# Modulation columns: the last gate of each layer summed over row tiles by VectorE, the first group of columns on a later unit

## The chip, the cores and the metric

One NeuronCore of a Trainium2 chip runs the whole program, one launch. The metric is the device time of one execution in microseconds (us). Before the change the median of three runs is 1773.07 us (1772.1 to 1774.9).

## The reference, cut to what matters

One inference step of a two-layer backbone. 128 context tokens and 256 latent tokens of width D = 1024 go through the same layers with different conditioning vectors (`c_ctx` and `c`). In each layer:

```python
mod = (silu(cond) @ w_mod[l] + b_mod[l]).reshape(B, 9, 1, 1024)
sh1, sc1, gt1, sh2, sc2, gt2, sh3, sc3, gt3 = [mod[:, i] for i in range(9)]
h = rmsnorm(x, g0) * (1 + sc1) + sh1;  x = x + 0.5 * gt1 * swiglu(h, w1[0], w2[0])
h = rmsnorm(x, g1) * (1 + sc2) + sh2;  x = x + gt2 * mixer(h)
h = rmsnorm(x, g2) * (1 + sc3) + sh3;  x = x + 0.5 * gt3 * swiglu(h, w1[1], w2[1])
```

The nine vectors sh1 to gt3 are the modulation. `w_mod[l]` is 1024 x 9216 in fp32. Vector i stands in columns i*D to (i+1)*D, so sh1 and sc1 are columns 0 to 2D, gt2 is 5D to 6D, and the last gate gt3 is 8D to 9D. It multiplies the output of the second feed-forward (FFN2), so it is needed when FFN2's second product comes out. Outputs are the normed tokens and the final states of the context scan. Everything is fp32.

## The kernel before, in words

**Main work.** Tokens are kept transposed, as 8 tiles `x0` to `x7` of 128 channels by 384 tokens. A weight unit is 512 KB (128 x 1024 fp32, mostly four row tiles by 256 columns). SyncE's queue (SP) loads it into `wr` (L149), ScalarE (ACT) copies the rounded high part to `wh` (L126), VectorE (DVE) subtracts to get the low part `wl` (L105), and TensorE (PE) runs three products per row tile and 128 columns, `mm3` (L198 to L200): high by high, high by low, low by high. A unit gives 24 matmuls. Units are prepared two ahead. The activations are split in the same way into `hh` and `hl`.

**Order.** PE follows the written program order. On DVE, ACT and the DMA queues a scheduler chooses the order when the program is built, by priority and by its own idea of times; each engine then runs its list strictly in order, and SP too. From the fourth unit on (`settled`) weight loads, and the loads of `mod_cols` and `mod_half`, carry a high priority (`ahead()`); the loads of `mod_wide` (L433) do not.

**Side work.** Everything but the big products is written as generators that are hung on `tracks`. `track(gen, rate, start)` sets a counter to -start*rate; after each unit `tick()` adds the rate, and each whole 1.0 lets the generator take one step. So rates and starts place the side work between the units.

**Modulation** is made in three ways.

- `mod_half`: columns 0 to 2D of layer 0, two halves, before and during the first units. Per row tile k one 512 KB load (L373; tiles k > 3 in another pool) and four matmuls (`band_products`, L356): silu(cond) against four column bands, each band into its own 32 rows of a bank.
- `mod_cols`: groups of up to 1536 columns (`MG`), two row tiles per step. A step loads two 128 x 1536 tiles (768 KB each, L394), one step ahead if `early_loads`, and then runs the four bands of each tile on PE (the trace records 16 matmuls per step). After four steps `mod_out` copies the bank out (ACT, L460), transposes it on PE and adds the bias.
- `mod_wide`: 1024 columns. Eight 512 KB loads (L433); for each row tile two accumulations on DVE, one per conditioning vector, `macc` (L123, 128 x 1024; the first row tile is done by ACT, L436); then PE sums over the 128 rows with eight small matmuls against a `pick` tile (L444, 16 records), and `mod_out`.

The loads of `modw` tiles share a pool of four buffers (`m6`): a load waits at the head of SP until the product or accumulation that read the buffer's last content is done.

**Norms.** Each residual update of `x` is followed by a square on ACT (L503) and an addition into `sqacc` on DVE (L105). When `x7` is done, PE sums `sqacc` over the channels (`token_sums`, L486), ACT and DVE make `rstd` (L522) and `diag` (L118), and PE broadcasts it (L533). PE meanwhile runs the next layer part's first products on the unnormed `xh`, `xl`.

**At the start**, PE first has the first half of columns 0 to 2D, then runs the products of row tiles 0 to 3 of units 0 and 1, with the second half's band products put between them; then it needs `hh4` to `hh7` (L639), which need the second half's scale `sc`.

Of the kernel before, what the change touches and what calls it, by code (L numbers as in the profile page):

```python
# [4 lines left out]

# [16 lines left out]
D = 1024  # L22
# [10 lines left out]
NMOD = 9  # L33
# [16 lines left out]
MG = 1536  # L50
# [6 lines left out]
def hybrid_step(ctx: ExitStack, tc: tile.TileContext, I, pos_r, pos_c, y_prompt, y_sample, new_state):  # L57
# [20 lines left out]
    def ax_bank():  # L78
        return ps_ax.tile([P, 512], F32, tag="ax", name="ax")
# [18 lines left out]
    def m6(shape, name, dt=F32):  # L98
        return mx.tile(shape, dt, tag="m6", name=name, bufs=4)
# [43 lines left out]
    def ahead():  # L143
        return nullcontext() if early["on"] else tc.high_priority()
# [73 lines left out]
    def track(gen, rate, start=0):  # L218
        tracks.append([gen, rate, -start * rate])
# [134 lines left out]
    def band_products(b, k, raw, w):  # L354
        for s in range(4):
            pe.matmul(  # L356
                b[32 * s : 32 * s + 32, :w],
                silu_c[:, k, :],
                raw[:, s * w : s * w + w],
                start=(k == 0),  # L360
                stop=(k == KD - 1),
                skip_group_check=True,
            )
# [21 lines left out]
    def mod_cols(l, c0, c1, early_loads=True):  # L385

        steps = [(c, min(MG, c1 - c), k) for c in range(c0, c1, MG) for k in range(0, KD, 2)]

        def load(c, n, k0):
            raws = []  # L390
            for k in (k0, k0 + 1):
                raw = m6([P, n], "modw")
                with ahead():
                    nc.sync.dma_start(raw, I["w_mod"][l][k * P : (k + 1) * P, c : c + n])  # L394
                raws.append(raw)
            return raws

        nxt = load(*steps[0]) if early_loads else None
        yield
        for i, (c, n, k0) in enumerate(steps):  # L400
            raws = nxt if early_loads else load(c, n, k0)
            if early_loads and i + 1 < len(steps):
                nxt = load(*steps[i + 1])
            yield
            if k0 == 0:
                b = ax_bank()
            for j in range(2):
                band_products(b, k0 + j, raws[j], n // 4)
            yield
            if k0 == KD - 2:  # L410
                yield from mod_out(l, b, [c + s * (n // 4) for s in range(4)], n // 4)
                mod_done(l, c, n)

    def mod_done(l, c0, n):

        for i in range(NMOD):
            if c0 < (i + 1) * D <= c0 + n:
                if i % 3 == 1:
                    norm_scale(l, i // 3)
                elif i % 3 == 2:  # L420
                    gate_scale(l, i // 3)
# [6 lines left out]
    def mod_wide(l, c0, n=WU):  # L428

        acc = [c4([P, WU], f"macc{s}") for s in range(2)]  # L430
        for k in range(KD):
            raw = m6([P, WU], "modw")
            nc.sync.dma_start(raw, I["w_mod"][l][k * P : (k + 1) * P, c0 : c0 + WU])  # L433
            for s in range(2):
                if k == 0:
                    act.activation(acc[s], raw, AF.Copy, scale=silu_c[:, k, s : s + 1])  # L436
                else:
                    stt(acc[s], raw, silu_c[:, k, s : s + 1], acc[s])
                yield
        w = WU // 4  # L440
        b = ax_bank()
        for i in range(2):
            for s in range(4):
                pe.matmul(  # L444
                    b[32 * s : 32 * s + 32, :w],
                    pick[:, i, :],
                    acc[i][:, s * w : (s + 1) * w],
                    start=(i == 0),
                    stop=(i == 1),
                    skip_group_check=True,  # L450
                )
        yield
        yield from mod_out(l, b, [c0 + s * w for s in range(4)], w)
        mod_done(l, c0, n)
        yield

    def mod_out(l, b, starts, w):
        nb = w // P
        ev = sp.tile([P, 512], F32, tag="c2", name="modev", bufs=7)
        act.activation(ev[:, :w], b[:, :w], AF.Copy)  # L460
        yield
        b2 = ax_bank()
        for j in range(nb):
            transpose(b2[:, j * P : (j + 1) * P], ev[:, j * P : (j + 1) * P], P)
        src = b2[:, :w].rearrange("p (b s r) -> p b s r", s=4, r=32)
        for s, c0 in enumerate(starts):
            j0 = c0 // P
            bias = bm_t[l][:, j0 : j0 + nb].unsqueeze(2).to_broadcast([P, nb, 2])
            add(mod_t[l][:, j0 : j0 + nb, :], src[:, :, s, 0:2], bias)
# [1195 lines left out]
    def mod_wides(l, c0, c1):  # L1665
        for c in range(c0, c1, WU):
            yield from mod_wide(l, c)

    def tables(l):
        if l == 0:  # L1670
            yield from s5_params(*s5_params_in(nc.gpsimd))
        yield from s5_tables(l)
# [97 lines left out]
    track(other_vectors(), 0.25, 8)  # L1770
    for l in range(DEPTH):
        if l == 0:
            track(mod_cols(0, 2 * D, 8 * D), 0.7)
            track(tables(0), 1.9, 8)
        else:
            track(tables(1), 1.6, 8)
            track(mod_cols(1, 6 * D, NMOD * D), 0.36, 10)
        nxt = Lead(l, 1)
        ffn(l, 0, 0, ld, nxt, None if l else more)
        ld, nxt = nxt, Lead(l, 2)  # L1780
        mixer(l, ld, nxt)
        if l == 0:
            track(mod_cols(0, 8 * D, NMOD * D, False), 1.0)
            track(mod_cols(1, 0, 2 * D, False), 0.5, 14)
            track(mod_wides(1, 2 * D, 6 * D), 1.2, 4)
        ld, nxt = nxt, Lead(l + 1, 0) if l + 1 < DEPTH else Final()
        ffn(l, 1, 2, ld, nxt)
        ld = nxt
# [59 lines left out]
```

## Time and profile before

| | |
|---|---|
| median of three runs | 1773.07 us |
| profiled execution | 1772.74 us |
| its span in the trace | 1770.9 us |
| mean granted clock of PE, share of full speed | 0.994 |
| PE / DVE / ACT busy, share of the span | 98% / 71% / 45% |
| DMA, mean over the span | 195 GB/s |

The span is the part that the trace covers; the execution's own time is 1.8 us longer. PE is busy nearly always. Where it is idle or runs at half clock is the first 50 us. One more matmul on PE, or one less, is therefore a change of the end, unless it falls into a wait.

### The profile page before, as it was taken

What the parts mean: (1) busy time and instruction counts of PE and PEld (TensorE: products, weight loads), DVE (VectorE), ACT (ScalarE), POOL (GpSimd) and SP (SyncE); (2) the same over time, 40 slices, a digit from 0 to 9 for tenths busy, and PEclk for the clock granted to TensorE, in tenths of its full rate; (3) what the DMA queues carried; (4) which work ended last, traced back from release to release, by engine and by line L of the source; (5) the groups of instructions that cost most, each with busy time, mean ns of one, the idle gap of its engine ahead of it and who ended that gap; (6) DMA issues with size and microseconds to landing.
All of it is one profiled execution on the core that took longest, in us unless ns stands there. A gap on an engine that the chain in (4) does not pass through costs nothing.

```text
span 1770.9 us, 31161 instructions
## 1 busy us (share of the span) xinstructions
PE 1739.2 (98%) x12244; PEld 1660.3 (94%) x12244; DVE 1249.3 (71%) x2352; ACT 795.7 (45%) x1332; POOL 202.6 (11%) x400
## 2 busy tenths in 40 slices
PE   6999999999999999999999999999999999999997
PEld 4989989999999999999999999999999999999997
DVE  5495776888986986657787666677699688544445
ACT  3344333475355553233367333335744546323233
POOL 2012333410010000000001133222100000000000
PEclk9999999999999999999999999999999999999999
DMA  9679787676753567766745577757666443444342
GB/s 358 209 234 317 251 261 213 204 213 188 251 150 102 185 223 247 255 197 219 250 131 184 174 220 233 244 172 236 167 209 195 131 126 113 135 128 128 122 125 77
DMA packets 250298, 344.49 MB, mean 195 GB/s; under 512 B 22016, under 2 KB 216268, under 8 KB 250153
## 3 DMA queue, kind: packets, MB, share of 16 engines
q1 hardware_dynamic: 225048, 299.18, 53.1%
q0 software_dynamic: 17088, 39.51, 7.4%
q10 hardware_dynamic: 8016, 3.82, 0.8%
q8 instruction: 96, 1.57, 0.4%
q14 instruction: 50, 0.40, 0.1%
HBM read 309.75 MB, written 32.70 MB: 193 GB/s over the span
## 4 chain that ended last, share of the span: by engine, by line
PE 84%; DVE 10%; DMA 2%; ACT 2%; issue 1%; DVEq 0%; SPq 0%; ACTq 0%
PE mm L198 26%; PE mm L200 26%; PE mm L199 26%; PE ax L356 3%; DVE wl L105 2%; DVE cacc L123 2%; PE tb L138 1%; DVE m_t L105 1%; DMA wr<-in_w_in_dram 1%; DVE m_hh L105 1%; DMA wr<-in_w_gate_dram 1%; ACT wh L126 1%; PE tb L1042 0%; DMA modw<-in_w_mod_dram 0%; DVE acc L105 0%
## 5 line engine op out<-in xcount | busy, mean ns | idle before, releaser
L105 DVE TENSOR_TENSOR wl<-wr,wh 128x1024 fp32r<-128x1024 f32 (+2 forms) x389 | 457.0, 1175 | 335.7 <-ACT wh L126 333.9
L126 ACT ACTIVATE wh<-wr 128x1024 fp32r<-128x1024 f32 (+1 forms) x387 | 395.9, 1023 | 629.1 <-PE mm L199 444.6
L198 PE MATMUL mm<-hh,wh 128*128 128x384 f32 x1840 | 625.7, 340 | 5.0 <-ACT hh L639 5.0
L200 PE MATMUL mm<-hh,wl 128*128 128x384 f32 x1840 | 618.6, 336 | 5.7 <-DVE wl L105 5.5
L199 PE MATMUL mm<-hl,wh 128*128 128x384 f32 x1840 | 617.7, 336 | 0.2
L198 PEld LDWEIGHTS mm<-hh,wh 128*128 128x128 f32 x1840 | 347.2, 189 | 21.8 <-ACT wh L126 7.5
L200 PEld LDWEIGHTS mm<-hh,wl 128*128 128x128 f32 x1840 | 347.0, 189 | 8.3 <-DVE wl L105 8.2
L199 PEld LDWEIGHTS mm<-hl,wh 128*128 128x128 f32 x1840 | 347.2, 189 | 1.1 <-DVE hl L105 1.0
L198 PE MATMUL mm<-ah,wh 128*128 128x384 f32 x800 | 273.1, 341 | 0.0
L200 PE MATMUL mm<-ah,wl 128*128 128x384 f32 x800 | 270.1, 338 | 0.0
L199 PE MATMUL mm<-al,wh 128*128 128x384 f32 x800 | 269.4, 337 | 0.0
L198 PEld LDWEIGHTS mm<-ah,wh 128*128 128x128 f32 x800 | 150.3, 188 | 6.4 <-ACT wh L126 2.3
L199 PEld LDWEIGHTS mm<-al,wh 128*128 128x128 f32 x800 | 150.4, 188 | 0.6
L200 PEld LDWEIGHTS mm<-ah,wl 128*128 128x128 f32 x800 | 150.2, 188 | 0.0
L123 DVE SCALAR_TENSOR_TENSOR x<-mm,gt,x 128x128 f32<-128x128 f32 x224 | 83.3, 411 | 37.2 <-PE mm L200 37.1
L123 DVE SCALAR_TENSOR_TENSOR macc<-modw,silu_c,macc 128x1024 f32<-128x1024 f32 x56 | 70.0, 1279 | 21.4 <-DMA modw<-in_w_mod_dram 21.4
L198 PE MATMUL mm<-xh,wh 128*128 128x386 f32 x240 | 84.0, 350 | 0.0
L199 PE MATMUL mm<-xl,wh 128*128 128x386 f32 x240 | 81.4, 339 | 0.0
L200 PE MATMUL mm<-xh,wl 128*128 128x386 f32 x240 | 81.3, 339 | 0.0
L126 ACT ACTIVATE ah<-av 128x384 fp32r<-128x384 f32 x82 | 41.9, 517 | 82.3 <-DVE av L105 82.2
L123 DVE SCALAR_TENSOR_TENSOR cacc<-pad,pv,cacc 128x399 f32<-128x399 f32 x120 | 69.6, 627 | 0.0
L105 DVE TENSOR_TENSOR av<-mm,sg 128x384 f32<-128x384 f32 x76 | 42.1, 555 | 23.3 <-PE mm L200 23.0
(315 smaller groups left out, 1838.9 us busy)
## 6 DMA issues: line engine op xcount, KB each, us to landing
wr<-in_ffn_w_dram SPq DMA_DIRECT2D x256, 512.0 KB, 3.8
modw<-in_w_mod_dram SPq DMA_DIRECT2D x56, 768.0 KB, 5.7
modw<-in_w_mod_dram SPq DMA_DIRECT2D x56, 512.0 KB, 4.6
wr<-in_w_gate_dram SPq DMA_DIRECT2D x48, 512.0 KB, 3.6
wr<-in_w_in_dram SPq DMA_DIRECT2D x24, 512.0 KB, 4.6
my<-my POOLq DMA_DIRECT2D x16, 512.0 KB, 5.5
ms<-ms POOLq DMA_DIRECT2D x16, 512.0 KB, 5.5
m_ms<-ms SPq DMA_DIRECT2D x16, 512.0 KB, 7.0
```

Source lines behind the costliest of these rows:

```text
L105: (eng or dve).tensor_tensor(out, a, b, op=op)
L123: dve.scalar_tensor_tensor(out, a, s, b, op0=op0, op1=op1)
L126: act.activation(hi, full, AF.Copy)
L138: pe.transpose(out, in_, ident[:rows, :rows])
L198: pe.matmul(out, wh[:, k, cols], xh, start=first, stop=False)
L199: pe.matmul(out, wh[:, k, cols], xl, start=False, stop=False)
L200: pe.matmul(out, wl[:, k, cols], xh, start=False, stop=last)
L356: pe.matmul(b[32 * s : 32 * s + 32, :w], silu_c[:, k, :], raw[:, s * w : s * w + w], start=(k == 0), stop=(k == KD - 1), skip_group_check= ...
```

## The change

In layer 0's first feed-forward, `mod_cols` of columns 2D to 8D is split: the first group (2D to 3.5D) starts three units later at rate 0.9, the rest runs from unit 18 on at rate 0.6 (before, all of it in a row from the beginning, at 0.7). Layer 0's gt3 is no longer made by `mod_cols` without early loads in FFN2, but by a `mod_wide` put in front of those for columns 2D to 6D of layer 1, on one track of rate 1.65 from the third unit. In layer 1, `mod_cols` ends at 8D instead of 9D, which leaves its last group 512 columns wide, and gt3 is made by a `mod_wide` in FFN2, which had no track.

```diff
-            track(mod_cols(0, 2 * D, 8 * D), 0.7)
+            track(mod_cols(0, 2 * D, 2 * D + MG), 0.9, 3)
+            track(mod_cols(0, 2 * D + MG, 8 * D), 0.6, 18)
             track(tables(0), 1.9, 8)
         else:
             track(tables(1), 1.6, 8)
-            track(mod_cols(1, 6 * D, NMOD * D), 0.36, 10)
+            track(mod_cols(1, 6 * D, 8 * D), 0.36, 10)
         ...
         if l == 0:
-            track(mod_cols(0, 8 * D, NMOD * D, False), 1.0)
+            track(chain(mod_wides(0, 8 * D, NMOD * D), mod_wides(1, 2 * D, 6 * D)), 1.65, 3)
             track(mod_cols(1, 0, 2 * D, False), 0.5, 14)
-            track(mod_wides(1, 2 * D, 6 * D), 1.2, 4)
+        else:
+            track(mod_wides(1, 8 * D, NMOD * D), 1.6, 3)
```

An import of `chain` at the top shifts all line numbers by one.

**SP at the start.** The queue of SyncE in the first 45 us, before. `modw_394` to `modw_400` are the loads of row tiles 4 to 7 of `mod_half`'s second half, `wr_416` and the following are units 2, 3, ..., and `modw_543` to `modw_579` the first four tiles of the first column group.

```order
L373 DMA modw_394<-in_w_mod_dram 128x2x512
L373 DMA modw_396<-in_w_mod_dram 128x2x512
L373 DMA modw_398<-in_w_mod_dram 128x2x512
L373 DMA modw_400<-in_w_mod_dram 128x2x512
L149 DMA wr_416<-in_ffn_w1_dram 128x4x256
L149 DMA wr_459<-in_ffn_w1_dram 128x4x256
L394 DMA modw_543<-in_w_mod_dram 128x1536
L394 DMA modw_545<-in_w_mod_dram 128x1536
L149 DMA wr_547<-in_ffn_w1_dram 128x4x256
L394 DMA modw_577<-in_w_mod_dram 128x1536
L394 DMA modw_579<-in_w_mod_dram 128x1536
```

The same place of the change; the group's first four tiles are now `modw_651` to `modw_687`, and unit 4 is `wr_543`.

```order
L374 DMA modw_394<-in_w_mod_dram 128x2x512
L374 DMA modw_396<-in_w_mod_dram 128x2x512
L395 DMA modw_651<-in_w_mod_dram 128x1536
L395 DMA modw_653<-in_w_mod_dram 128x1536
L395 DMA modw_685<-in_w_mod_dram 128x1536
L395 DMA modw_687<-in_w_mod_dram 128x1536
L374 DMA modw_398<-in_w_mod_dram 128x2x512
L374 DMA modw_400<-in_w_mod_dram 128x2x512
L150 DMA wr_416<-in_ffn_w1_dram 128x4x256
L150 DMA wr_459<-in_ffn_w1_dram 128x4x256
L150 DMA wr_543<-in_ffn_w1_dram 128x4x256
```

The group's four loads are issued after the fourth unit in the program, where loads have a high priority, and so stand ahead of the second half's last two tiles and of units 2, 3 and 4 in the queue. They need the same buffers as before: each waits for the band products of one of the second half's row tiles 0 to 3.

**ACT at the start.** ScalarE's list from `modev` (the copy-out of the second half's bank) to `hh4`, before.

```order
L126 ACTIVATE wh_382<-wr_380 128x1024
L126 ACTIVATE wh_418<-wr_416 128x1024
L460 ACTIVATE modev_503<-ax_440 128x256
L126 ACTIVATE wh_461<-wr_459 128x1024
L639 ACTIVATE hh4_519<-xr_402 128x384
```

The same of the change.

```order
L127 ACTIVATE wh_382<-wr_380 128x1024
L461 ACTIVATE modev_503<-ax_440 128x256
L127 ACTIVATE wh_418<-wr_416 128x1024
L127 ACTIVATE wh_461<-wr_459 128x1024
L127 ACTIVATE wh_545<-wr_543 128x1024
L640 ACTIVATE hh4_519<-xr_402 128x384
```

Three units are now converted between `modev` and `hh4`, where one was. On DVE the low parts of units 2 and 3 stand between the bias additions and the scale in the same way.

**DVE at the end of layer 0's mixer.** VectorE's list from the residual update of `x6` to `rstd`, before.

```order
L123 SCALAR_TENSOR_TENSOR x6_107<-mm_7032,gt01_119,x6_107 128x128
L123 SCALAR_TENSOR_TENSOR x6_107<-mm_7032,gt01_119,x6_107 128x256
L123 SCALAR_TENSOR_TENSOR xl_7100<-x6_107,sc02_114,xh_7099 128x128
L105 TENSOR_TENSOR sqacc_6907<-sqacc_6907,sq_7096 128x384
L123 SCALAR_TENSOR_TENSOR xl_7100<-x6_107,sc02_114,xh_7099 128x256
L123 SCALAR_TENSOR_TENSOR x7_108<-mm_7033,gt01_119,x7_108 128x128
L123 SCALAR_TENSOR_TENSOR x7_108<-mm_7033,gt01_119,x7_108 128x256
L105 TENSOR_TENSOR wl_7126<-wr_7123,wh_7125 128x1024
L105 TENSOR_TENSOR sqacc_6907<-sqacc_6907,sq_7109 128x384
```

The same of the change, with two accumulations of the gate among them.

```order
L124 SCALAR_TENSOR_TENSOR x6_107<-mm_7032,gt01_119,x6_107 128x128
L124 SCALAR_TENSOR_TENSOR x6_107<-mm_7032,gt01_119,x6_107 128x256
L124 SCALAR_TENSOR_TENSOR macc0_7313<-modw_7563,silu_c_109,macc0_7313 128x1024
L106 TENSOR_TENSOR sqacc_6907<-sqacc_6907,sq_7096 128x384
L124 SCALAR_TENSOR_TENSOR xl_7100<-x6_107,sc02_114,xh_7099 128x128
L124 SCALAR_TENSOR_TENSOR xl_7100<-x6_107,sc02_114,xh_7099 128x256
L124 SCALAR_TENSOR_TENSOR x7_108<-mm_7033,gt01_119,x7_108 128x128
L106 TENSOR_TENSOR wl_7126<-wr_7123,wh_7125 128x1024
L124 SCALAR_TENSOR_TENSOR x7_108<-mm_7033,gt01_119,x7_108 128x256
L124 SCALAR_TENSOR_TENSOR xl_7113<-x7_108,sc02_114,xh_7112 128x128
L124 SCALAR_TENSOR_TENSOR macc1_7314<-modw_7563,silu_c_109,macc1_7314 128x1024
L106 TENSOR_TENSOR sqacc_6907<-sqacc_6907,sq_7109 128x384
```

Of the gate's 14 accumulations two stand behind the update of `x6`, and the last addition into `sqacc` comes after both. Six stand earlier, spread over the fifteen units before, four around `diag` right behind `rstd`, and two some units later. Layer 1 has the same list at its mixer's end.

## Rows read from the trace of the kernel before

**Rows 1.** The page's part 1: busy time, share and instructions of each engine.

```profile
PE 1739.2 (98%) x12244; PEld 1660.3 (94%) x12244; DVE 1249.3 (71%) x2352; ACT 795.7 (45%) x1332; POOL 202.6 (11%) x400
```

**Rows 2.** Windows: us, busy of PE, PEld, DVE, ACT, POOL (instructions), clock, DMA share, GB/s.

```profile
30.00:40.00 10.00, 10.00 (x92) 6.67 (x88) 2.37 (x4) 2.23 (x3) 0.00 (x0) 1.00 1.05 385
...
600.00:620.00 20.00, 20.00 (x117) 20.00 (x116) 16.35 (x33) 13.24 (x24) 0.00 (x0) 1.00 0.40 122
```

**Rows 3.** Timeline of PE around four modulation steps: start us, us, instruction.

```profile
58.81 0.34 PE L200 MATMUL mm<-hh,wl 128*128 128x384 f32 x1
59.08 1.50 PE L356 MATMUL ax<-modw,silu_c 128*32 128x384 f32 x16
...
60.79 0.34 PE L199 MATMUL mm<-hl,wh 128*128 128x384 f32 x1
...
630.00 0.34 PE L200 MATMUL mm<-xh,wl 128*128 128x386 f32 x1
...
631.54 0.35 PE L199 MATMUL mm<-xl,wh 128*128 128x386 f32 x1
...
702.07 0.33 PE L200 MATMUL mm<-ah,wl 128*128 128x384 f32 x1
...
703.61 0.34 PE L199 MATMUL mm<-al,wh 128*128 128x384 f32 x1
...
791.06 0.34 PE L200 MATMUL mm<-hh,wl 128*128 128x384 f32 x1
...
792.18 0.34 PE L199 MATMUL mm<-hl,wh 128*128 128x384 f32 x1
```

**Rows 4.** Timeline of PE, the second half of the first columns.

```profile
37.69 1.07 PE L356 MATMUL ax<-modw,silu_c 128*32 128x256 f32 x16
...
39.84 0.38 PE L138 MATMUL ax<-ident,modev 128*128 128x128 f32 x2
43.28 0.69 PE L198 MATMUL mm<-hh,wh 128*128 128x384 f32 x1 [3.05 <-ACT hh L639]
...
49.62 0.34 PE L198 MATMUL mm<-hh,wh 128*128 128x384 f32 x1
```

**Rows 5.** Timeline of SP's DMA issues at the start (us: first to last of a row).

```profile
14.28 10.21 SPq L373 DMA_DIRECT2D modw<-in_w_mod_dram  x8
...
30.24 2.16 SPq L394 DMA_DIRECT2D modw<-in_w_mod_dram  x2
...
32.97 1.72 SPq L394 DMA_DIRECT2D modw<-in_w_mod_dram  x2
```

**Rows 6.** Timeline of ACT at the start.

```profile
36.17 1.06 ACT L126 ACTIVATE wh<-wr 128x1024 fp32r<-128x1024 f32 x1 [8.14 <-DMA wr<-in_ffn_w_dram]
...
42.70 1.10 ACT L639 ACTIVATE hh<-xr 128x384 fp32r<-128x384 f32 x2 [2.54 <-DVE xr L120]
```

**Rows 7.** Timeline of DVE at the start and at the end of layer 0's mixer.

```profile
40.26 0.30 DVE L105 TENSOR_TENSOR mod<-ax,bm 128x4 f32<-128x4 f32 x3 [1.78 <-PE ax L138]
40.48 1.21 DVE L105 TENSOR_TENSOR wl<-wr,wh 128x1024 fp32r<-128x1024 f32 x1
...
41.79 0.17 DVE L123 SCALAR_TENSOR_TENSOR sc<-mod,pv 128x8 f32<-128x8 f32 x1
...
614.39 0.74 DVE L123 SCALAR_TENSOR_TENSOR x<-mm,gt,x 128x128 f32<-128x128 f32 x2
...
618.53 0.55 DVE L105 TENSOR_TENSOR sqacc<-sqacc,sq 128x384 f32<-128x384 f32 x1
```

**Rows 8.** Timeline of PE where layer 0's second feed-forward begins.

```profile
620.61 0.37 PE L486 MATMUL ax<-ones,sqacc 128*32 128x1 f32 x24
...
625.26 0.81 PE L533 MATMUL ax<-diag,ones 128*128 128x384 f32 x2
```

**Rows 9.** The tile macc: ns min/median/max of its accumulations; idle before them by releaser (us, times).

```profile
L123 DVE SCALAR_TENSOR_TENSOR macc<-modw,silu_c,macc x56: 1270/1278/1287, 648.1 to 865.8; 128x1024 f32<-128x1024 f32 x56
...
DMA modw<-in_w_mod_dram: 29.3, 17
```

More of the change, by code (lines that the diff above doesn't have):

```diff
@@ L3 @@
 from functools import partial
+from itertools import chain
 from contextlib import ExitStack, nullcontext
```

## The prediction, made before the changed kernel ran

> **What bounds the kernel now.** I read the busy times first: PE is busy in 98% of the span [rows 1]. Then I read the windows: in 600 to 620 us PE is busy in all of 20.00 us, with 117 regular products, so one takes 20.00 / 117 = 0.171 us; DVE has 3.65 us left there [rows 2]. So nearly everywhere PE's own list is the bound: what the change takes off that list comes off the end, and what makes PE wait goes on it. Third, the timeline of the first 50 us, the one place where PE is not the bound: it stands 3.05 us for `hh` at 43.28, and then 18 products take until 49.62, 6.34 / 18 = 0.35 us each, twice the 0.171 [rows 2, 4]. DMA moves 385 GB/s there, with a busy share of 1.05 [rows 2]: that stretch is full of transfers, and a load that is put in front delays all those behind it.
>
> **Taken off PE.** The cost of a modulation step is read from the distance between the starts of two regular products around it, less the two spacings of 0.171 that would be there anyway. With 1536 columns: 60.79 - 58.81 - 0.34 = 1.64 us. With 1024: 631.54 - 630.00 - 0.34 = 1.20 us. With 512: 792.18 - 791.06 - 0.34 = 0.78 us. The sum over rows by `pick`: 703.61 - 702.07 - 0.34 = 1.20 us [rows 3]. Layer 0's gt3 loses four steps of 1024 columns and gains one `pick`: 4 x 1.20 - 1.20 = 3.6 us. In layer 1 the last four steps shrink from 1536 to 512 columns, and one `pick` comes in: 4 x (1.64 - 0.78) - 1.20 = 2.2 us. Transposes are as many as before. These places lie between products where PE has no pause, so all of it counts: **-5.8 us**. The split of layer 0's columns in FFN1 moves its steps to other units and leaves their number; PE has room for none and loses none there, so I cost it at 0, within 1 us.
>
> **Added to DVE and ACT.** In each layer 14 accumulations of 1.278 us [rows 9], 17.9 us, and two on ACT. The bytes loaded are the same as before. DVE is not the bound on average, so this is free as far as nothing that PE awaits stands behind it. Twice it does, below. Behind 650 us the picks stand as close to their last accumulation as those of before, and I cost them at 0.
>
> **The start.** The words of the change say later, but SP's list says earlier: four loads of 768 KB now stand ahead of the last two tiles of `mod_half`'s second half and of units 2, 3 and 4. They can go only when the buffers come free, which depends on PE's band products and so falls at the same times as before: two were issued in 30.24 to 32.40, two in 32.97 to 34.69 [rows 5]. Before, the eight loads of L373 were all issued by 24.49 [rows 5]. When does the last tile now land? Unit 2 landed at 36.17 [rows 6]; at 385 GB/s a 512 KB load takes 0.524 / 0.385 = 1.36 us, so tile 7 of the second half landed at about 34.8 and tile 5 at 32.1. From there the stream now carries 4 x 0.786 = 3.15 MB first, 8.2 us, to 40.3. Tile 7 lands two loads later, at 43.0; units 2, 3 and 4 at 44.4, 45.7 and 47.1. Before, PE ran the products of tiles 6 and 7 at 37.69, 2.9 us after the data was there [rows 4]; so that slack is gone and PE stops.
>
> What follows is a chain through DVE and ACT. Tile 7's product ends at 43.5 (half of 1.07 [rows 4]); six regular products after the pause, at 0.35, to 45.6; the transposes and the first bias addition (before, 39.84 to 40.26: 0.4 us [rows 4, 7]) to about 46.1. Then, by the new order, DVE makes unit 2's low part, 1.2 us [rows 7], the other bias additions, 0.3, and unit 3's low part, whose high part ACT has at 45.7 + 1.1 = 46.8 [rows 6]: to 48.8. From `sc` to `hh` it was 42.70 - 41.79 = 0.9 [rows 6, 7]; so `hh4` starts at 49.7. ACT has unit 4's high part done at 47.1 + 1.1 = 48.2, before that. PE follows `hh` by 43.28 - 42.70 = 0.6, so it resumes at 50.3 in place of 43.28: **+7.0 us**. The half-clock stretch that follows is there in both. The bounds: if the engines moved a tenth more than in that row and the six products ran at full clock, +5; if the first load started a microsecond late and the band products ran at half clock too, +8.5.
>
> The Trainium skill (DMA: Bandwidth & Descriptors, Specifications) gives a fabric ceiling of 435 GB/s and a limit per core on HBM of about 358 GB/s. The row of 385 lies above the second and below the first; by the first, the estimate of the stretch would be some 1.5 us shorter, and by the second some 1 us longer. Neither changes the sign.
>
> **The end of each mixer.** PE's `token_sums` at 620.61 wait for the last addition into `sqacc`, which ended at 618.53 + 0.55 = 619.08: a slack of 1.5 us [rows 7, 8]. Two accumulations now stand between the update of `x6` at 614.39 and that addition, and there is no pause of DVE left to hide them, since what precedes is tied to PE's last products. Adding up the new list from 614.39: `x6` 0.74, accumulation 1.28, addition 0.5, two `xl` 0.75, half of `x7` 0.37, a low part 1.2, the other half 0.45, `xl` 0.35, accumulation 1.28, addition 0.55, together 7.5, ends at 621.9; 2.8 us later, and past the slack by 1.3. That is the lower bound. Six further accumulations lie ahead; four of them, 5.1 us, fall in the stretch in which DVE had 3.65 us free [rows 2], of which about 1 us comes after the sums. If nothing else gives, DVE enters 614.39 up to 2.4 us late, which puts the upper bound at 3.7. Low parts have several microseconds of slack before their products, so most of the lateness can be made up; I take 0.5 of it, nearer to the lower end: **+1.8 us**. Then `rstd` and, with one accumulation before it, `diag` come at about 626.2, while PE asks for it at 625.26 + 1.8 = 627.1 [rows 8]: no second wait. Layer 1 has the same list, so **+3.6 us** for both. A wait of this length may or may not lower PE's clock; in the likeliest case it does not, since regular products stand right behind the sums.
>
> **Sum.** -5.8 + 7.0 + 3.6 = +4.8 us. The profiled execution took 1772.74 us, so 1777.5; the median of the runs lies 0.3 higher, so **1777.9 us**.
>
> **Rivals.**
>
> 1. *The queue's order costs nothing at the start, and DVE fills only gaps.* For it: the change's own words, later loads, and DVE's 71%. It needs tile 7 to land before about 37.7 and the accumulations to find free time. Then only the work taken off counts: 1773.1 - 5.8 = 1767.3, faster. Against it: the loads' waits and the 385 GB/s. It decides if tile 7's load is issued ahead of the group's after all, or lands before 38 us. Chance 0.10.
> 2. *Only the start costs.* The scheduler's gap filling works, the last addition into `sqacc` keeps within its slack. -5.8 + 7 = +1.2, with a start of 5 even -0.8: 1772.3 to 1774.3, no measurable change. For it: 1.5 us of slack; against it: two accumulations are 2.56 us. Chance 0.27.
> 3. *The accumulations stall DVE.* Before, accumulations waited for their tiles 29.3 us in 17 cases, 1.7 us each [rows 9], and DVE's list is strict. If one such wait falls between the residual updates of each mixer's end, PE waits 1.8 + 1.7 = 3.5 us, and a pause of that length brought half clock at 43.28: 18 products at 0.35 in place of 0.171, 3.2 us [rows 2, 4]. That makes -5.8 + 7 + 2 x 6.7 = +14.6, 1787.7. For it: loads of the gate now stand between weight loads at a place where DVE was full; against it: DMA is at 122 GB/s around 600 us [rows 2], so tiles land soon. Chance 0.15.
>
> The forecast itself has 0.48, its own range is +2 to +9: 1775 to 1782. About 0.2% (3.5 us) is what a measurement can tell from no change. Faster by more than that: 0.11, rival 1 and a little of 2. Within it: 0.30, rival 2 and the lower end of the forecast. Slower: 0.59. The range leaves out rival 1 and the upper part of rival 3: 1770 to 1786.
>
> **What the profile will show.** Right: PE idle for 4 to 5 us before the band products at 38 to 43, with the modulation load as releaser, and the first `hh` of the second half near 49.7 on ACT; the group's loads on SP at 30 to 35 ahead of two L374 loads; `token_sums` with a wait of 1 to 3 us on `sqacc` at both mixers' ends, some 6 us after the old place in layer 0; the steps of 1024 columns gone from 630 to 660 us. Wrong: tile 7's product still at 37.7; no wait at the sums; or an `hh` of the mixers' end that comes late by more than the sums do. The work taken off PE is the surest term; if the end comes out faster than 1770, the start is what I misread.

## The result, and the profile after

The changed kernel takes 1784.53 us (median of four, 1783.47 to 1786.25), against 1773.99 us for the kernel before in the same comparison. The ratio is 1.0067, 95% interval 1.0054 to 1.0079: slower, by about 10.5 us. The forecast was 1777.9 in a range of 1770 to 1786. The direction and the two places of the loss were right; both losses were larger than I had put them, one of them came by another wait, and a third, small one was not forecast.

The changed kernel's span is 1781.7 us. PE's busy time answers to [rows 1]: 1.7 us less than before, in a span that is 10.8 us longer, so the loss is idle time of PE and not more work.

```profile
span 1781.7 us, 31143 instructions
PE 1737.5 (98%) x12212; PEld 1660.2 (93%) x12212; DVE 1278.3 (72%) x2384; ACT 801.0 (45%) x1337; POOL 202.9 (11%) x400
```

**The start.** SP's issues in the changed kernel; they answer to [rows 5]. First column: start; second: from first to last issue of the row.

```profile
14.52 6.63 SPq L374 DMA_DIRECT2D modw<-in_w_mod_dram  x6
30.72 4.39 SPq L395 DMA_DIRECT2D modw<-in_w_mod_dram  x4
35.16 0.99 SPq L374 DMA_DIRECT2D modw<-in_w_mod_dram  x2
36.20 25.51 SPq L150 DMA_DIRECT2D wr<-in_ffn_w_dram  x7
```

The last two tiles of the second half go at 35.16, where before all eight were gone by 24.49. SP stands from 21 to 31 us, because the head of its queue waits for buffers. PE's rows of the same stretch answer to [rows 4].

```profile
42.75 0.64 PE L357 MATMUL ax<-modw,silu_c 128*32 128x256 f32 x8 [4.51 <-DMA modw<-in_w_mod_dram]
44.12 1.08 PE L357 MATMUL ax<-modw,silu_c 128*32 128x256 f32 x8 [0.73 <-DMA modw<-in_w_mod_dram]
...
47.22 0.63 PE L139 MATMUL ax<-ident,modev 128*128 128x128 f32 x2
52.32 0.69 PE L199 MATMUL mm<-hh,wh 128*128 128x384 f32 x1 [4.47 <-ACT hh L640]
```

PE waits 4.51 us for the first of the two tiles, and the new wait stands ahead of the old one for `hh`, which has grown from 3.05 to 4.47 us. PE goes on at 52.32 in place of 43.28. ACT in that stretch, answering to [rows 6]:

```profile
45.27 0.38 ACT L461 ACTIVATE modev<-ax 128x256 f32<-128x256 f32 x1 [16.75 <-PE ax L357]
45.59 1.06 ACT L127 ACTIVATE wh<-wr 128x1024 fp32r<-128x1024 f32 x1
47.15 1.06 ACT L127 ACTIVATE wh<-wr 128x1024 fp32r<-128x1024 f32 x1 [0.50 <-DMA wr<-in_ffn_w_dram]
49.58 1.06 ACT L127 ACTIVATE wh<-wr 128x1024 fp32r<-128x1024 f32 x1 [1.38 <-DVE wl L106]
51.74 1.10 ACT L640 ACTIVATE hh<-xr 128x384 fp32r<-128x384 f32 x2 [1.10 <-DVE xr L121]
```

Three high parts stand between `modev` and `hh`, as the order had shown. The first follows `modev` at once, the second waits 0.50 us for its weights, the third 1.38 us for a low part on DVE. `hh` itself then waits another 1.10 us for DVE (`xr`), so it is DVE's list that holds it in the end.

**The mixers' ends.** The waits of PE in the whole of the changed kernel: total us, times, longest us. Before, the waits for low parts were 5.5 us in 7 with the longest 1.4.

```profile
PE mm L199 <- ACT hh L640: 6.5, 2, 4.5
PE mm L201 <- DVE wl L106: 6.4, 6, 1.8
PE ax L357 <- DMA modw<-in_w_mod_dram: 5.7, 3, 4.5
...
PE ax L487 <- DVE sqacc L106: 4.6, 5, 1.4
```

The new wait of 1.8 us for a low part is in the mixer's output product, 40 us ahead of the place where I had looked. PE's rows there:

```profile
592.75 0.33 PE L200 MATMUL mm<-hl,wh 128*128 128x384 f32 x1
594.89 0.44 PE L201 MATMUL mm<-hh,wl 128*128 128x384 f32 x1 [1.80 <-DVE wl L106]
...
596.50 0.52 PE L200 MATMUL mm<-hl,wh 128*128 128x384 f32 x1
596.82 0.53 PE L201 MATMUL mm<-hh,wl 128*128 128x384 f32 x1
```

After the wait, products start 0.32 us apart from 596.50 on, in place of 0.17: half clock. The windows (us; busy of PE, PEld, DVE, ACT, POOL; clock; DMA share; GB/s) show it, and show DVE with hardly a free moment from 580 to 600:

```profile
580.00:590.00 10.00, 10.00 (x60) 10.00 (x59) 9.96 (x18) 4.45 (x6) 0.00 (x0) 1.00 0.53 160
590.00:595.00 5.00, 3.20 (x19) 2.88 (x19) 4.97 (x10) 2.94 (x4) 0.00 (x0) 1.00 0.71 227
595.00:600.00 5.00, 5.00 (x20) 5.00 (x21) 5.00 (x9) 0.99 (x2) 0.00 (x0) 0.66 0.87 290
600.00:605.00 5.00, 5.00 (x31) 5.00 (x30) 4.31 (x19) 2.27 (x4) 0.00 (x0) 1.00 0.82 232
```

What took DVE's time is seen a little earlier. DVE's rows around the first two of the gate's accumulations, and the low part that PE waited for:

```profile
578.09 1.29 DVE L124 SCALAR_TENSOR_TENSOR macc<-modw,silu_c,macc 128x1024 f32<-128x1024 f32 x1 [0.86 <-DMA modw<-in_w_mod_dram]
579.29 0.55 DVE L106 TENSOR_TENSOR gt<-mm,gt 128x384 f32<-128x384 f32 x1
579.75 1.28 DVE L124 SCALAR_TENSOR_TENSOR macc<-modw,silu_c,macc 128x1024 f32<-128x1024 f32 x1
...
593.62 1.22 DVE L106 TENSOR_TENSOR wl<-wr,wh 128x1024 fp32r<-128x1024 f32 x1
594.75 1.02 DVE L106 TENSOR_TENSOR acc<-acc,gt 128x384 f32<-128x384 f32 x2
```

The first accumulation makes DVE stand 0.86 us for its tile, and the two take 2.6 us. Before, DVE stood idle here for 0.92 and 0.96 us, so part of this falls into free time. Behind it come the merges of the branches (`gt`, `gate_b`, `acc`), the `hl` and low parts, nearly back to back until 600, and the rest is not made up: the low part starts at 593.62, which is 11.70 us later than before, while the products ahead of it are 9.62 us late. So 2.1 us are left. The rows of before show what the low part could bear; it ended at 583.13, 0.17 us ahead of its product:

```profile
581.92 1.21 DVE L105 TENSOR_TENSOR wl<-wr,wh 128x1024 fp32r<-128x1024 f32 x1
...
583.30 0.34 PE L200 MATMUL mm<-hh,wl 128*128 128x384 f32 x1
```

The gate's two accumulations on ACT end at 574.4, and ACT stands idle for 0.97 and 3.12 us before its next two high parts, so it isn't they that make the low part late.

**The account.** The 8832 regular products of the two traces stand in the same order, so the lag of the change behind the kernel before can be read at each. PE resumes 9.0 us late at 52.32. Of this 0.5 is there already at 37.9, ahead of the first new wait (the ten experiments have -0.3 to 2.4 there). The half-clock stretch behind it is 13 products long in place of 18 and gives back 0.8, which leaves +8.3. In the first feed-forward the lag swings with the moved steps, and is 8.4 when all are done, at 360; the norm at its end adds 1.5 (a wait of 0.82 us for `sqacc` at 371.57 and one of 0.36 us for `diag`), to 9.9 at 377, and small shifts take 0.3; the output product of layer 0's mixer adds 3.6 and its token sums 0.6, to 13.8; the steps taken off FFN2 give back 4.8, the pick and small shifts cost 1.4, to 10.5; layer 1's FFN1 gives back 3.6; waits elsewhere in layer 1's mixer give 0.5; layer 1's output product and sums cost 2.1 and 0.6; its pick and small shifts cost 1.3. At the last product it is 10.35, and the measured difference is 10.5.

### The profile page after: what moved, and what is told of

Read it like the earlier page. It is cut to its first block, busy times and chain, and to the rows that moved or that the text cites. A ratio compares the mean times of both kernels' runs of the same rounds, so it can differ in the third digit from the quotient of the medians.

```text
span 1781.7 us, 31143 instructions
## 1 busy us (share of the span) xinstructions
PE 1737.5 (98%) x12212; PEld 1660.2 (93%) x12212; DVE 1278.3 (72%) x2384; ACT 801.0 (45%) x1337; POOL 202.9 (11%) x400
## 4 chain that ended last, share of the span: by engine, by line
PE 77%; DVE 13%; DMA 5%; ACT 3%; issue 2%; SPq 0%; DVEq 0%; ACTq 0%
PE mm L199 24%; PE mm L201 24%; PE mm L200 24%; DVE wl L106 3%; DVE cacc L124 2%; PE ax L357 2%; DMA wr<-in_w_gate_dram 2%; DVE m_t L106 2%; PE tb L139 1%; DMA modw<-in_w_mod_dram 1%; DMA wr<-in_w_in_dram 1%; ACT wh L127 1%; DVE m_hh L106 1%; DVE acc L106 1%; DMA wr<-in_ffn_w_dram 1%
## 5 line engine op out<-in xcount | busy, mean ns | idle before, releaser
L124 DVE SCALAR_TENSOR_TENSOR macc<-modw,silu_c,macc 128x1024 f32<-128x1024 f32 x84 | 105.1, 1278 | 17.2 <-DMA modw<-in_w_mod_dram 17.2
L696 ACT ACTIVATE sg<-mm 128x384 f32<-128x384 f32 x76 | 36.6, 482 | 47.2 <-PE mm L201 47.1
```

What stands on the lines that cost most here:

```text
L124: dve.scalar_tensor_tensor(out, a, s, b, op0=op0, op1=op1)
L696: act.activation(t, bg[m][:, :NT], AF.Silu)
```

## The experiments

Each was compared with the kernel before on the same chip. The before medians were 1772.8 to 1773.0 us.

**1. The split alone (`split_only`).** Before, with

```diff
-            track(mod_cols(0, 2 * D, 8 * D), 0.7)
+            track(mod_cols(0, 2 * D, 2 * D + MG), 0.9, 3)
+            track(mod_cols(0, 2 * D + MG, 8 * D), 0.6, 18)
```

> Layer 0's columns split and restarted as in the change, the gates as before. Theory (two separate causes: the split costs the start, the accumulations cost the mixers' ends): the split alone carries nearly all of the loss, the start +8.5 us and the end of the first feed-forward +1.5 us, so about 1784, and PE resumes near 52 us with hh as releaser. Rival 1 (the prediction's size): +7 us, 1781. Rival 2 (the loss lies in the accumulations and the start is made good later): under +3 us, below 1777.

Measured: 1784.23 us, ratio 1.0059 (1.0046 to 1.0072), +10.5 us. The theory's +10 is inside the interval (+8.2 to +12.8), 7 is not. PE's two waits are those of the change, 5.13 us for the tile and 4.50 us for `hh`:

```profile
43.36 1.08 PE L356 MATMUL ax<-modw,silu_c 128*32 128x256 f32 x8 [5.13 <-DMA modw<-in_w_mod_dram]
...
52.98 0.69 PE L198 MATMUL mm<-hh,wh 128*128 128x384 f32 x1 [4.50 <-ACT hh L639]
```

**2. The gates alone (`gates_only`).** The change, with the two lines above put back to one.

> The two gates by accumulation, and the tracks that go with them; layer 0's columns as before. Theory: work taken off PE -6 us, and a loss of 3.9 us (layer 0) and 2.7 us (layer 1) at the mixers' ends: +0.5 us, 1774 to 1775, with waits of PE on wl of about 1.8 us in the output products near 585 and 1448 us. Rival 1 (the prediction's size, waits at the token sums only): -2.2 us, 1772. Rival 2 (accumulations fill gaps): -5.8 us, 1768.

Measured: 1773.33 us, ratio 1.0003 (0.9994 to 1.0011): no change. The work taken off PE and the waits at the mixers' ends cancel, and both are in the trace: 1.94 us for the low part and 0.54 us at the sums of layer 0.

```profile
584.40 0.44 PE L201 MATMUL mm<-hh,wl 128*128 128x384 f32 x1 [1.94 <-DVE wl L106]
...
623.97 0.37 PE L487 MATMUL ax<-ones,sqacc 128*32 128x1 f32 x24 [0.54 <-DVE sqacc L106]
```

So the net loss of the change is the split's; the gates alone neither gain nor lose.

**3. The first group's loads issued before the high priority begins (`group_start_1`).**

```diff
-            track(mod_cols(0, 2 * D, 2 * D + MG), 0.9, 3)
+            track(mod_cols(0, 2 * D, 2 * D + MG), 0.9, 1)
```

> The change with one number different: the first column group starts one unit late in place of three, so that its loads are issued before the loads get their high priority; in the queue they come behind all of the second half's loads and unit 2 to 4. Theory (queue order): the start's 8.5 us are gone, 1775 to 1776; PE resumes near 43.5 us. Rival (the new spacing of the group's products costs, whatever the queue's order): 1782 or more, at most 2 us better than the change.

Measured: 1773.36 us, ratio 1.0006 (0.9996 to 1.0017); 11 us better than the change, and somewhat below the theory's 1775 to 1776. In SP's queue the four loads now stand behind the second half's eight and units 2 to 4, and PE goes on after a wait of 3.06 us, as before. That it goes on at 44.83 and not at 43.28 is a lag of 1.55 us that is there already before the wait, at 37.4, in this execution (with 1777.69 us the slowest of the twelve):

```profile
44.83 0.69 PE L199 MATMUL mm<-hh,wh 128*128 128x384 f32 x1 [3.06 <-ACT hh L640]
```

**4. The change's own start, without the high priority of those four loads (`group_plain_loads`).** This separates the place in the queue from the time of the start, which experiment 3 had both moved.

```diff
-                with ahead():
+                with (nullcontext() if c == c0 and k0 < plain else ahead()):
                     nc.sync.dma_start(raw, I["w_mod"][l][k * P : (k + 1) * P, c : c + n])
...
-            track(mod_cols(0, 2 * D, 2 * D + MG), 0.9, 3)
+            track(mod_cols(0, 2 * D, 2 * D + MG, plain=4), 0.9, 3)
```

> The change with the start of its first group untouched (third unit), but that group's first four loads without the high priority; in the queue they then come behind the second half's last tiles and units 2 to 4. Theory (it is the queue's order, not the group's later start): as group_start_1, 1773 to 1776, PE resumes at 43 to 44 us. Rival (the later start itself): 1782 or more.

Measured: 1773.64 us, ratio 1.0010 (1.0000 to 1.0021). The start is three units late as in the change, and its cost is gone. SP's issues with it:

```profile
25.52 5.66 SPq L150 DMA_DIRECT2D wr<-in_ffn_w_dram  x3
31.27 1.16 SPq L395 DMA_DIRECT2D modw<-in_w_mod_dram  x1
38.89 3.65 SPq L150 DMA_DIRECT2D wr<-in_ffn_w_dram  x2
42.63 0.46 SPq L395 DMA_DIRECT2D modw<-in_w_mod_dram  x1
...
47.90 0.97 SPq L395 DMA_DIRECT2D modw<-in_w_mod_dram  x2
```

PE goes on with `hh` at 43.73:

```profile
43.73 0.44 PE L199 MATMUL mm<-hh,wh 128*128 128x384 f32 x1 [3.06 <-ACT hh L640]
```

It is the place in the queue. The products of the group still run at the later units, and cost nothing that can be seen by that: the lag behind before is -0.5 us where the products after 43.73 are through, near 50, and -0.4 near 352.

**5. The rest from unit 18 (`rest_from_18`).** Before, with the first group on its old track.

```diff
-            track(mod_cols(0, 2 * D, 8 * D), 0.7)
+            track(mod_cols(0, 2 * D, 2 * D + MG), 0.7)
+            track(mod_cols(0, 2 * D + MG, 8 * D), 0.6, 18)
```

> Layer 0's first group exactly as before; only the other columns of the group's track start at unit 18 at rate 0.6; gates as before. Theory (the loss at the end of the first feed-forward comes with these late columns, whose loads and steps now reach into it): +0.5 to +1.5 us, 1773.5 to 1774.5, with a wait of about 0.8 us at the token sums near 362 us. Rival (it comes with the late start of the first group): no change, no new wait there.

Measured: 1774.16 us, ratio 1.0005 (0.9996 to 1.0014). The timing doesn't tell +0.9 from nothing. The trace has a wait at the end of the first feed-forward that the kernel before doesn't have, but at `diag`, not at the sums:

```profile
364.08 0.37 PE L486 MATMUL ax<-ones,sqacc 128*32 128x1 f32 x24
369.74 0.88 PE L533 MATMUL ax<-diag,ones 128*128 128x384 f32 x2 [0.86 <-DVE diag L118]
```

So the late columns do reach into that place, by about a microsecond. The other traces bear it out. Between the products that stand at 351.6 and 367.2 us before, this run loses 1.2 us, the six others with the columns from unit 18 (the change among them, with 1.5) lose 1.1 to 2.7, also where the start costs nothing (experiments 3, 4 and 10: 1.2, 1.1, 1.1); the four runs without them (2, 6, 7 and 8) lose 0.0. So most of the change's 1.5 us there is theirs.

**6. The gates' accumulations held until after the norm (`gates_held`).** As `gates_only`, with the accumulations reading a copy of silu(cond) that depends on the last normed tile:

```diff
+            sl = cst.tile([P, KD, 2], F32, tag=f"silu_h{l}", name=f"silu_h{l}")
+            late = hold.hs[7][1].bitcast(F32)[:, : 2 * KD].rearrange("p (k s) -> p k s", s=2)
+            stt(sl, late, 0.0, silu_c[:, :, :2])
...
-                    stt(acc[s], raw, silu_c[:, k, s : s + 1], acc[s])
+                    stt(acc[s], raw, sl[:, k, s : s + 1], acc[s])
```

> Gates by accumulation as in gates_only, but the accumulations read a copy of silu(cond) that depends on the feed-forward's last normed tile, so none can run before about 640 us (and its like in layer 1); their start is one unit later. Theory (place of the accumulations): the mixers' ends are as before and the work taken off PE remains, -5.5 to -6 us, 1768 to 1769. Rival (the amount of added DVE work costs, wherever it stands): within 1.5 us of gates_only, 1773 to 1776.

Measured: 1765.76 us, ratio 0.9958 (0.9945 to 0.9971), 7.2 us faster than before. The same DVE work is done; only its place differs. PE's waits for low parts are down to 3.2 us in 4, none of them at the mixers' ends:

```profile
PE mm L201 <- DVE wl L106: 3.2, 4, 1.4
PE ax L492 <- DVE sqacc L106: 2.8, 2, 1.4
```

The token sums start at 620.94 without a wait, where before they were at 620.61. The gain is 1.2 us more than the theory's 6, within the interval (-9.8 to -5.1).

**7. Held until x0 (`gates_held_x0`).** One line of experiment 6 differs, and the order shows four accumulations before the sums, none between `x6` and the last addition into `sqacc`.

```diff
-            late = hold.hs[7][1].bitcast(F32)[:, : 2 * KD].rearrange("p (k s) -> p k s", s=2)
+            late = x[0][:, : 2 * KD].rearrange("p (k s) -> p k s", s=2)
```

> As gates_held, but the copy depends on the updated x0, so that accumulations may run from the first residual update of the mixer's end on; the two that stood before it are moved behind, four of 14 stand before the token sums, none between x6 and the last addition into sqacc. Theory (the loss came from the two accumulations ahead of the merge of the branches, which made a low part late): nearly all is kept, 1766 to 1768, no wait on wl near 585 and 1448 us. Rival (the prediction's: any accumulations in the mixer's end make the token sums late): 1.5 to 2 us per layer lost, 1769 to 1771, waits at the sums.

Measured: 1765.64 us, ratio 0.9963 (0.9951 to 0.9975): all of it kept. Neither the output product nor the sums wait. Accumulations in the mixer's end are covered, if they stand neither ahead of the branches' merge nor behind `x6`: the update of `x6` comes 1.3 us late, and the 1.5 us of slack at the sums [rows 7, 8] take that up.

**8. Held until x5 (`gates_held_x5`).** The same line with `x[5]`. The list of DVE from `x6` on is now that of the change, and almost nothing stands before it, so the wait that the prediction had added up can be seen by itself.

> As gates_held_x0, but the copy depends on the updated x5. The list of DVE from x6 to the last addition into sqacc is then that of the change, with two accumulations in it, and only one stands before. Theory (the prediction's adding-up of that list, which the change itself could not show since PE had already been held back by the late low part): PE waits 1.3 us at the token sums of each layer, 2.6 us in all, so 1768 to 1769. Rival (accumulations there are covered, and the 0.5 us seen in the change is all): 1 us or less in all, 1765 to 1767.

Measured: 1768.64 us, ratio 0.9977 (0.9966 to 0.9988), by the medians 3.0 us more than with `x[0]`, by the ratios 2.5; the two intervals overlap a little, so the size rests on the traces. The sums wait, in layer 0 and in layer 1, and against the trace of experiment 7 the products behind them lose 1.2 us each (the profiled execution is also 2.6 us behind from the first 40 us on, and loses another 1.2 at layer 1's first norm; the edit touches neither place):

```profile
624.49 0.37 PE L492 MATMUL ax<-ones,sqacc 128*32 128x1 f32 x24 [1.13 <-DVE sqacc L106]
...
1483.17 0.37 PE L492 MATMUL ax<-ones,sqacc 128*32 128x1 f32 x24 [1.14 <-DVE sqacc L106]
```

DVE's rows before the first of them are the list that was added up:

```profile
617.67 0.73 DVE L124 SCALAR_TENSOR_TENSOR x<-mm,gt,x 128x128 f32<-128x128 f32 x2
618.33 1.27 DVE L124 SCALAR_TENSOR_TENSOR macc<-modw,silu_h,macc 128x1024 f32<-128x1024 f32 x1
...
622.70 1.27 DVE L124 SCALAR_TENSOR_TENSOR macc<-modw,silu_h,macc 128x1024 f32<-128x1024 f32 x1
623.89 0.55 DVE L106 TENSOR_TENSOR sqacc<-sqacc,sq 128x384 f32<-128x384 f32 x1
```

From `x6` at 617.67 to the end at 624.44 it took 6.8 us; the prediction had 7.5. The update of `x6` itself comes 0.6 us late, behind the one accumulation that stands ahead of it. So of the 1.13 us of wait about half is the list's excess over the slack (6.8 - 4.7 before - 1.5 = 0.6) and half is that lateness.

**9. The change, with the gates held (`split_gates_held`).** The split as in the change, the hold of experiment 6.

> The change with its gates held until after the norm (as in gates_held) and the split as it is. Theory (two independent causes): the change's time less what holding gave against gates_only, 7.5 us: 1776 to 1778. Rival (the slow start lets later work catch up, so that both don't add): 1773 or less.

Measured: 1777.46 us, ratio 1.0022 (1.0013 to 1.0031). By the ratios holding takes 0.0045 off the change (1.0067 to 1.0022) and 0.0045 off `gates_only` (1.0003 to 0.9958). The two causes add.

**10. Held, and the group from the first unit (`held_and_start_1`).** Experiments 3 and 6 together.

> gates_held with layer 0's columns as in group_start_1 (the split kept, first group from the first unit). Theory (independent causes): the sum of the two, -7.2 and about +0.5, so 1766 to 1767.5. Rival (the later spread of the columns gains too, since it takes a wait of 1.1 us out of the first feed-forward): 1765 or less.

Measured: 1765.45 us, ratio 0.9960 (0.9948 to 0.9971). It doesn't differ from experiment 6; the split gains nothing with or without its fault. Its theory (1766 to 1767.5) and its rival (1765 or less) leave a gap into which it falls. The kernels of experiments 6, 7 and 10 beat the kernel before by about 7 us and the change by about 19.

## Why the prediction was right, and where its sizes failed

**The number.** 1784.53 us lies in the stated range, but above the forecast's own, 1775 to 1782; the stated range reached to 1786 for a part of rival 3. Three terms came out larger than forecast, by 1.3, 1.5 and 3.3 us, and the fourth missed by 0.2 only, so that the number is in the range is in part luck. What was understood beforehand is the start, and the work taken off PE.

**Work taken off PE: -5.8 forecast, right.** Read between the products, layer 0's FFN2 lost 4.8 and got 1.2 for the pick, layer 1 lost 3.6 and got 1.2: -6.0. It is visible as a gain only when the accumulations don't disturb (experiment 6).

**The start: +7.0 forecast, 8.3 measured in the trace.** The chain was right: the place in the queue (experiments 3 and 4), the tile that lands late, the bias additions behind two low parts. PE resumed at 52.32, not 50.3. Tile 7's product ended at 45.2, not 43.5: it began at 44.12 instead of 43.0, and took 1.08 us instead of half of that. The shorter half-clock stretch, which I had taken to be the same in both, gave 0.8 back, so the term was too small by 1.3. The landing was worked out on a stream of 385 GB/s [rows 2], but the engines ran dry while SP stood at its head, to 57 GB/s in the first two microseconds after the loads could go:

```profile
30.00:32.00 2.00, 2.00 (x19) 1.31 (x22) 1.63 (x4) 0.00 (x0) 0.00 (x0) 1.00 0.31 57
32.00:34.00 2.00, 2.00 (x22) 1.25 (x14) 0.00 (x0) 0.00 (x0) 0.00 (x0) 1.00 0.87 329
```

I had let the new loads join a stream that was still full. The bound of +8.5, for a late first load and band products at half clock, is nearest to what came: the first load went 0.48 us later than before, and tile 7's product ran at half clock. Behind that, the transposes, the low parts and `hh` took 47.22 to 52.32, 5.1 us; the prediction had 4.7, from 45.6 to 50.3.

**The first feed-forward: 0 within 1 us forecast, +1.5.** The columns moved to its end cost something at the norm behind it, some 1.1 us or more wherever they are late (experiment 5). This was the part that I had dismissed because the number of steps is the same.

**The mixers' ends: +3.6 forecast, +6.9 measured (4.2 and 2.7), by another wait.** This step failed as I had put it: "Low parts have several microseconds of slack before their products, so most of the lateness can be made up". No row stood behind that sentence, and the trace of before contradicts it: the low part in question had 0.17 us. Of the six earlier accumulations four were counted as one sum against DVE's free time between 600 and 620 us, and two not at all; but two of the six stand ahead of the merge of the branches, at 578 us, where DVE then has hardly a pause until 600. They made the output product's low part 2.1 us later, and PE waited there. In layer 0 half clock followed, which I had held unlikely because regular products stand right behind such a wait; here they did too. Since PE was late by then, the sums behind had only 0.5 us left to wait, in place of the 1.8 forecast, and they started 14 us behind the old place in layer 0, not 6. Taken by itself the forecast wait exists: 1.2 us per layer against a forecast of 1.8 (experiment 8). That this comes near the lower bound of 1.3 is luck, since the list was 0.7 us shorter than added up and `x6` came 0.6 us late. Experiment 7 shows that accumulations between `x0` and `x6`, for which I had added 0.5 us, cost nothing as long as none stands behind `x6`.

**The rivals.** Rival 1, that the words "one unit later" hold for the queue, was wrong: the queue's order decided. Rival 2, that only the start costs, has its case in experiment 9, where the accumulations cost nothing: about 4 us slower than before, and not 1.2, since the start and the late columns cost more than its 7. Rival 3 had the mechanism that was measured: a pause of PE from a late DVE, followed by half clock; it had the place of the residual updates, not of the branches' merge.

## What to carry to other kernels

A start that is moved later in the program can come earlier in a queue, when a priority changes on the way: read the queue's own order, and ask of each load that moves ahead which loads of others stand behind it and whether it can go at all when its turn comes. Work that is to fill an engine's gaps has to be checked stretch by stretch, since a free quarter of the whole span is no room at the one place where the engine is full; there, in the change, two accumulations cost 3.6 and 2.1 us (layer 0 and 1), the twelve others 0.6 in each. A list's cheap place can be forced by making the work depend on something that exists only after the critical stretch.

## What the runs showed of the hardware

A pause of PE of 1.80 us in an otherwise full stretch was followed by a granted clock of 0.66 in the window 595 to 600 us (the level of 1.2 GHz in part of it, products 0.32 us apart in place of 0.17), beginning 1.3 us after the pause and costing 1.6 us on top of it. With `gates_only` the pause of 1.94 us at 584.40 did the same (0.66 in the window 585 to 590 us). In layer 1 a pause of the same 1.80 us was not followed by it:

```profile
1455.00:1460.00 5.00, 3.46 (x20) 3.46 (x21) 5.00 (x8) 1.31 (x3) 0.00 (x0) 1.00 0.88 297
1460.00:1465.00 5.00, 5.00 (x31) 5.00 (x30) 5.00 (x16) 2.22 (x5) 0.00 (x0) 1.00 0.84 268
```

So the same wait cost 3.6 us in one place and 2.1 in the other, its own 1.80 included. Its length doesn't decide: pauses of 2.08 us (585.45) and 2.48 us (1446.62) in the same two places of experiment 4 were not followed by half clock; the granted clock was 1.00 in the ten microseconds behind them. The runs don't show what made the difference.
